# Bilinear einsum: the last weight group in three transfers of five, two and one rows instead of four transfers of four, two, one and one

## The chip, the cores and the metric

The kernel runs on one core of one Trainium2 chip. Times are microseconds of the device for one execution. A span, read from a profile, is about 1.3 us shorter than the time of the same execution. A ratio here is the mean time of one kernel's fast runs over that of the other kernel's fast runs of the same rounds, so it is not quite the ratio of the medians that are quoted. An interval is a 95% interval.

## The reference

```python
batch, dim_i, dim_j, dim_k = 32, 256, 256, 128      # all float32
out = np.einsum('bi,bj,kij->bk', x, y, weight)
```

The weight has 128 x 256 x 256 float32 values, 33.6 MB, and has to be read once. The other inputs and the output are small.

## The kernel before

The 128 values of k are cut into 32 groups of four. In a group, a partition holds one k and eight consecutive values of i, the eight "rows" of 256 weights. For each row one matmul multiplies by a block form of x and adds up in PSUM; after the eight rows VectorE multiplies with y and sums. The weights come by transfers that GpSimd issues and that convert to bf16 on the way (33.62 MB are read from HBM; the queue of these thirty groups moved 15.73 MB, half of their 31.46 MB of float32); two groups (0 and 16) come as float32 through another queue (2.11 MB). Each transfer has its own semaphore, and the first matmul that needs a row waits for it.

```python
LOADS = (
    ((8, 24), 0, 8),                  # groups, first row, row after the last
    ((4, 12, 20, 28), 0, 8),
    (tuple(range(2, 32, 4)), 0, 8),
    (tuple(range(1, 32, 4)), 0, 8),
    ((3, 11, 19, 27), 0, 8),
    ((7, 23), 0, 8),
    ((15,), 0, 8),
    ((31,), 0, 4),
    ((31,), 4, 6),
    ((31,), 6, 7),
    ((31,), 7, 8),
)
# ... cut ...
    sw = [
        nc.gpsimd.dma_start(
            out=w_of(groups)[:, :, lo * J:hi * J],
            in_=rows_of(groups)[:, :, lo * J:hi * J],
        ).then_inc(s, 16).ins
        for (groups, lo, hi), s in zip(LOADS, s_w)
    ]
# ... cut: all of these are issued at the start, back to back ...
            for g in unit[o:o + n]:
                s = sem_of.get((g, ic))
                if s is not None and s.num not in landed:
                    landed.add(s.num)
                    need.append(s)
# ... cut: the matmul of this row waits for what is in need ...
            done(v.tensor_tensor_reduce(
                out=prod[:, 0, :], in0=sums[:, 0, :], in1=y4, scale=1.0, scalar=0.0,
                op0=mult, op1=add, accum_out=acc[:, unit[0]:unit[0] + 1],
            )._wait_ge(s_pe, n_pe))
# ... cut ...
    sp.dma_start(out=out_v, in_=acc)._wait_ge(s_dve, n_dve).then_inc(s_out, 16)
```

Of the kernel before, what the change touches and what calls it, by code (L numbers as in the profile page):

```python
# [22 lines left out]
    ((3, 11, 19, 27), 0, 8),  # L23
    ((7, 23), 0, 8),
    ((15,), 0, 8),
    ((31,), 0, 4),
    ((31,), 4, 6),
    ((31,), 6, 7),
    ((31,), 7, 8),
)  # L30

# [315 lines left out]
```

## Time and profile before

| | before |
|---|---|
| time, median of 6 runs | 84.94 us (84.89 to 85.02) |
| span of the profiled execution | 83.4 us |
| TensorE busy, VectorE busy | 32.6 us (39%), 24.8 us (30%) |
| read from HBM | 33.62 MB, 404 GB/s over the span |
| transfers issued by GpSimd | 11 |

No compute engine is busy for half of the span, while the rate is nearly constant (203 to 218 GB/s written in slices 5 to 38 of 40); the prediction shows the slices and the chain of waits that say so. Two groups of the page are of use later. Their columns are: line, engine, operation, what it writes and reads, shapes, count; then busy us and mean ns of one; then the idle time of the engine before them, with what ended it.

```profile
L120 POOL DMA_DIRECT2D w_sb<-in_weight_dram x11 | 7.5, 700 | 0.6 <-issue 0.6
L301 DVE CUSTOM_DVE_ANT_0 tmp<-ps,y 128x256 f32<-128x256 f32 x2 | 0.9, 426 | 1.6 <-PE ps L236 1.4
```

The first says that issuing all eleven transfers keeps GpSimd busy for 7.5 us at the start. The second is the multiply-and-sum of groups 15 and 31; of its idle time, 1.4 us were spent waiting for TensorE's last matmul, so VectorE has that much to spare at the end.

### The profile page before, as it was taken

The page shows a single profiled execution, that of the slowest core. Times are in us where ns is not written, and L with a number is a line of the kernel's source. Part 1 is how long each engine was busy: PE and PEld are TensorE (multiplying, and loading weights), DVE is VectorE, ACT ScalarE, POOL GpSimd, SP SyncE. Part 2 cuts the span into 40 slices and gives each one's busy share as a digit, 9 for nine tenths or more (in the row PEclk, how much of TensorE's full clock was granted, in tenths as well). Part 3 has the DMA queues.
Part 4 walks back from the last instruction along what each step waited for, and adds up shares of the span by engine and source line. Part 5 has one row for each costly group of instructions (what it writes and reads, how often), then busy time and mean ns, then how long its engine had stood idle before and what let it go on. Part 6 is the DMA issues. An engine that isn't in the chain of part 4 may idle for free.

```text
span 83.4 us, 257 instructions
## 1 busy us (share of the span) xinstructions
PE 32.6 (39%) x136; PEld 4.3 (5%) x43; DVE 24.8 (30%) x28; ACT 5.3 (6%) x5; POOL 8.2 (10%) x17
## 2 busy tenths in 40 slices
PE   0000000000000000000099999997009999995780
PEld 0000000000000000000000000000000100112330
DVE  0038595000000000000000000002999900899932
ACT  0039830000000000000000000000000000000000
POOL 5999300000000000000000000000000000000000
PEclk9999999999999999999999999999995699999999
DMA  3999999999999999999999999999999999999980
GB/s 126 383 360 311 216 216 214 210 214 218 214 218 210 214 212 218 218 216 212 212 212 218 216 218 210 214 212 218 216 214 210 218 212 216 218 214 208 203 120 8
DMA packets 4928, 17.91 MB, mean 215 GB/s; under 512 B 384, under 2 KB 832, under 8 KB 4672
## 3 DMA queue, kind: packets, MB, share of 16 engines
q0 software_dynamic: 4400, 15.73, 94.3%
q1 hardware_dynamic: 432, 2.11, 6.7%
q10 hardware_dynamic: 96, 0.07, 0.3%
HBM read 33.62 MB, written 0.02 MB: 404 GB/s over the span
## 4 chain that ended last, share of the span: by engine, by line
DMA 47%; PE 39%; DVE 6%; another core or an unknown queue 2%; POOL 2%; issue 2%; POOLq 0%
DMA w_sb<-in_weight_dram 47%; PE ps L236 39%; DVE tmp L293 5%; POOL w_sb L120 2%; DVE tmp L301 1%; POOL const-float32-0.0 L331 0%; POOLq L331 0%; POOL const-uint8-127 L331 0%; POOL const-float32-1.0 L331 0%; DVE acc L301 0%
## 5 line engine op out<-in xcount | busy, mean ns | idle before, releaser
L236 PE MATMUL ps<-w_sb,xblk 128*128 128x512 bf16 (+1 forms) x136 | 32.6, 398 | 48.7 <-DMA w_sb<-in_weight_dram 43.9
L293 DVE TENSOR_TENSOR tmp<-ps,y 128x4096 f32<-128x4096 f32 (+3 forms) x4 | 8.6, 2153 | 48.4 <-PE ps L236 48.4
L297 DVE TENSOR_REDUCE acc<-tmp 128x16 f32<-128x4096 f32 (+3 forms) x4 | 8.6, 2155 | 0.1
L236 PEld LDWEIGHTS ps<-w_sb,xblk 128*128 128x128 bf16 x43 | 4.3, 101 | 76.9 <-DMA w_sb<-in_weight_dram 42.7
L120 POOL DMA_DIRECT2D w_sb<-in_weight_dram x11 | 7.5, 700 | 0.6 <-issue 0.6
L177 ACT CAST w_sb<-w_f 128x1024 bf16<-128x1024 f32 x4 | 4.0, 1042 | 0.4 <-DMA w_f<-in_weight_dram 0.4
L191 DVE COPY x_rep<-x_sb 32x1024 f32<-32x1024 f32 x1 | 0.7, 724 | 5.6 <-PEq L331 5.6
L226 DVE STREAM_TRANSPOSE y<-y_rep 32x256 f32<-32x256 f32 x4 | 1.7, 435 | 0.1
L197 DVE STREAM_TRANSPOSE xt<-x_rep 32x256 f32<-32x256 f32 x4 | 1.7, 434 | 0.1
L177 ACT ACT_TABLE_LOAD x1 | 1.3, 1283 | 5.5 <-PEq L331 5.5
L209 DVE TENSOR_SCALAR xblk<-xt,mask 128x256 bf16<-128x256 f32 x4 | 1.4, 501 | 0.0
L301 DVE CUSTOM_DVE_ANT_0 tmp<-ps,y 128x256 f32<-128x256 f32 x2 | 0.9, 426 | 1.6 <-PE ps L236 1.4
L221 DVE COPY y_rep<-yt 32x1024 f32<-32x1024 f32 x1 | 0.7, 682 | 0.0
L204 DVE TENSOR_REDUCE mask<-ident 128x4 f32<-128x128 f32 x1 | 0.4, 380 | 1.0 <-POOL ident L168 1.0
L218 DVE STREAM_TRANSPOSE yt<-y_sb 32x256 f32<-32x256 f32 x1 | 0.4, 446 | 0.0
L168 POOL TENSOR_SCALAR_AFFINE_SELECT ident<-ident 128x128 f32<-128x128 f32 x1 | 0.3, 287 | 0.1
L167 POOL MEMSET ident<- 128x128 f32 x1 | 0.3, 289 | 0.0
L301 DVE DVE_READ_ACCUMULATOR2_ANT acc<- 128x1 f32 x2 | 0.2, 84 | 0.0
L331 POOL MEMSET const-float32-0.0<- 128x1 f32 x1 | 0.1, 99 | 0.2 <-issue 0.2
L331 POOL MEMSET const-bfloat16-1.0<- 128x1 bf16 x1 | 0.1, 102 | 0.0
L331 POOL MEMSET const-uint8-127<- 128x1 uint8 x1 | 0.1, 102 | 0.0
L331 POOL MEMSET const-float32-1.0<- 128x1 f32 x1 | 0.1, 99 | 0.0
## 6 DMA issues: line engine op xcount, KB each, us to landing
w_sb<-in_weight_dram POOLq DMA_DIRECT2D x2, 4096.0 KB, 48.5
w_sb<-in_weight_dram POOLq DMA_DIRECT2D x2, 2048.0 KB, 43.6
w_f<-in_weight_dram SPq DMA_DIRECT2D x2, 1024.0 KB, 6.9
w_sb<-in_weight_dram POOLq DMA_DIRECT2D x2, 1024.0 KB, 41.2
w_sb<-in_weight_dram POOLq DMA_DIRECT2D x1, 512.0 KB, 72.6
w_sb<-in_weight_dram POOLq DMA_DIRECT2D x1, 256.0 KB, 73.3
w_sb<-in_weight_dram POOLq DMA_DIRECT2D x1, 128.0 KB, 73.4
w_sb<-in_weight_dram POOLq DMA_DIRECT2D x2, 64.0 KB, 73.1
```

Of the source, the lines that this page charges most:

```text
L120: nc.gpsimd.dma_start(out=w_of(groups)[:, :, lo * J:hi * J], in_=rows_of(groups)[:, :, lo * J:hi * J],).then_inc(s, 16).ins
L177: c = act.copy(out=w_sb[:, place_of[g], lo:hi], in_=w_f[:, n, lo:hi])
L191: t = done(v.tensor_copy(out=x_rep, in_=x_sb.rearrange("b (ip ic) -> b ic ip", ic=IC).unsqueeze(3) .to_broadcast([B, IC, IP, KK]),)._wait_ ...
L197: c = v.transpose(out=xt[q * 32:(q + 1) * 32, :, :], in_=x_rep[:, :, q * IP // Q:(q + 1) * IP // Q, :],)
L204: t = done(v.tensor_reduce(out=mask, in_=ident.rearrange("p (ip kk) -> p kk ip", kk=KK), axis=AX, op=add,)._wait_ge(s_pool, 2))
L209: c = v.tensor_scalar(out=xblk[:, :, :, kk], in0=xt, scalar1=mask[:, kk:kk + 1], scalar2=None, op0=mult,)
L221: t = done(v.tensor_copy(out=y_rep, in_=yt.unsqueeze(3).to_broadcast([B, J // 32, B, KK]),)._wait_ge(s_dve, t))
L226: c = v.transpose(out=y4[q * 32:(q + 1) * 32, :].rearrange("p (jb j) -> p jb j", j=32), in_=y_rep[:, :, q * BQ:(q + 1) * BQ, :],)
L236: return pe.add_instruction(mybir.InstMatmult(name=nc.get_next_instruction_name(), engine=mybir.EngineType.PE, ins=[pe.lower_ap(rhs), pe.l ...
L293: t = done(v.tensor_tensor(out=prod, in0=sums, in1=y4.unsqueeze(1).to_broadcast([P, n_g, J]), op=mult,)._wait_ge(s_pe, n_pe))
L297: done(v.tensor_reduce(out=acc[:, unit[0]:unit[-1] + 1:unit[1] - unit[0]], in_=prod, axis=AX, op=add,)._wait_ge(s_dve, t))
L301: done(v.tensor_tensor_reduce(out=prod[:, 0, :], in0=sums[:, 0, :], in1=y4, scale=1.0, scalar=0.0, op0=mult, op1=add, accum_out=acc[:, uni ...
```

## The change

The intent is to save one transfer on a stream that does not rest (the DMA engines are at 90% or more in slices 2 to 38 of 40), while the last transfer stays small, so that little work is left when it lands.

```diff
     ((15,), 0, 8),
-    ((31,), 0, 4),
-    ((31,), 4, 6),
-    ((31,), 6, 7),
+    ((31,), 0, 5),
+    ((31,), 5, 7),
     ((31,), 7, 8),
 )
```

## The prediction

The sum came to minus 0.047 us, from 85.0 to 84.95 us.

> **What bounds the kernel now.** I first read the busy shares by slice, to see which resource never rests, and then the chain of work that ended last, in order of time, to see what sets the end. The page of the kernel before has this:
>
> ```profile
> PE   0000000000000000000099999997009999995780
> ...
> PEclk9999999999999999999999999999995699999999
> DMA  3999999999999999999999999999999999999980
> GB/s 126 383 360 311 216 216 214 210 214 218 214 218 210 214 212 218 218 216 212 212 212 218 216 218 210 214 212 218 216 214 210 218 212 216 218 214 208 203 120 8
> ```
>
> Each digit is a slice of 83.4 / 40 = 2.1 us. The DMA engines are full from the second slice to the thirty-eighth; TensorE starts half way and has gaps afterwards. The rate counts what is written, in bf16; what is read is float32, twice that, so the flat 210 to 218 GB/s is about 430 GB/s of reading. The kernel is a weight stream, and its time is the stream, plus what must be done after its last byte.
>
> That tail is the last part of the chain (start in us, length in us, what):
>
> ```profile
> 74.81 1.19 another core or an unknown queue
> 76.00 0.04 issue
> 76.04 1.89 PE ps L236 x8
> 77.93 0.53 another core or an unknown queue
> 78.46 0.04 issue
> 78.50 1.03 PE ps L236 x8
> 79.53 0.18 another core or an unknown queue
> 79.71 0.04 issue
> 79.75 0.60 PE ps L236 x4
> 80.35 0.06 another core or an unknown queue
> 80.41 0.05 issue
> 80.45 0.59 PE ps L236 x3
> 81.04 0.01 another core or an unknown queue
> 81.06 0.05 issue
> 81.10 0.30 PE ps L236
> 81.40 0.02 issue
> 81.42 0.43 DVE tmp L301
> ```
>
> There is only one core, so "another core or an unknown queue" is not that. Every one of these waits is TensorE waiting for a weight transfer that was issued about 73 us earlier, too long ago for the view to tie them together; the matmuls that end them are the ones that carry a wait on a piece's semaphore. So the start of each "issue" line is the moment at which a piece has landed: groups 7 and 23 at 76.00, group 15 at 78.46, then of group 31 rows 0 to 3 at 79.71, rows 4 and 5 at 80.41, and row 7 at 81.06. Row 6 does not show as a wait in the chain; the weight load that opens it starts at 80.75 in the order of instructions, so it landed at about 80.71. (A "row" is one of the eight rows of 256 weights that a partition holds of a group: 128 x 256 x 4 = 131,072 bytes read, one matmul.) After 81.06 come 0.04 of wake-up, the last matmul, the multiply-and-sum on VectorE, and the store, which ends the span at 83.4, that is 2.3 us later.
>
> [...] the fit below gives 131,072 B in 0.302 us, 434 GB/s. [...] Here the pieces are queued behind each other[...]: two one-row pieces landed within 0.65 us together. [...] (eight take 1.03 us, and one by itself 0.27: 0.76 / 7 = 0.109). [...] the digits 5 and 6 in the clock row are one such half-speed stretch in this trace.
>
> **The change part by part.** It removes one transfer (pieces 4, 2, 1, 1 become 5, 2, 1), one semaphore and one wait of TensorE. The bytes, the 136 matmuls, their order, VectorE's work and the store stay, which the comparison of the two programs' instructions per engine confirms: the only difference beside line numbers is one DMA fewer on GpSimd's queue.
>
> What a piece costs on the stream: group 15 is eight rows in one piece, 78.46 - 76.00 = 2.46 us. Group 31 is the same eight rows in four pieces, 81.06 - 78.46 = 2.60 us. Three more pieces cost 0.14 us, so **a piece costs 0.047 us**, and a row (2.46 - 0.047) / 8 = 0.302 us. Check: four rows give 4 x 0.302 + 0.047 = 1.25 (seen 79.71 - 78.46 = 1.25); two rows 0.65 (seen 0.70); two pieces of one row 0.70 (seen 0.65). Single landings scatter by 0.05 around the fit, but their sum holds.
>
> The new landings follow, as estimates from these two numbers:
> - rows 0 to 4: 78.46 + 5 x 0.302 + 0.047 = 80.02
> - rows 5 and 6: 80.02 + 2 x 0.302 + 0.047 = 80.67
> - row 7: 80.67 + 0.302 + 0.047 = 81.01 or 81.02, against 81.06
>
> What TensorE does with them, with 0.04 us from landing to start and 0.109 us from one matmul to the next: rows 0 to 4 start between 80.06 and 80.50, and TensorE could take row 5 at 80.61; it lands at 80.67 and starts at 80.71, row 6 at 80.82, and TensorE could take row 7 at 80.93. Row 7 starts only when it has landed, at 81.06. So the last piece still ends the chain, with 0.13 us to spare; before, row 6 started at 80.75, row 7 could have gone at 80.86, and went at 81.10, 0.24 us to spare. The larger first piece eats 0.11 us of slack, not of time. After row 7's start everything is as before.
>
> The sum on the path that sets the end: **minus 0.047 us** for one piece, and nothing else. The wait removed on TensorE (0.04 or 0.05 us of wake-up) lay in time that TensorE had to spare. On GpSimd one issue fewer saves about 0.55 to 0.7 us (eleven issues took 548 to 884 ns, median 696) at about 8 us; it brings forward the identity, VectorE's mask and the block weights by up to that, but TensorE waits for weights until 41.9 us, so none of it reaches the end. 85.0 - 0.05 gives 84.95 us.
>
> **The rivals.**
>
> First: a piece costs much more than 0.047 us, [...] the 0.2 us that one would get by adding up packet times. [...] I give it little.
>
> Second: the coarser first piece turns the tail from waiting for DMA to waiting for TensorE. Five matmuls begin 0.31 us later than four did. If TensorE ran at half its clock in the last 1.5 us, 256 columns would take 0.22 us each, and the eight matmuls, from 80.06, would start the last at 80.06 + 7 x 0.22 = 81.6, that is 0.5 us later than now: 85.5 us. In this trace the clock is full from slice 33 on, and the half-speed stretch (matmuls at half rate in about 62.8 to 66.2 us) is far ahead of the tail with a second one only after the last matmul. [...] the three runs before, within 0.13 us, show no such outlier. At full clock this rival is worth 0 us, since 0.13 us of slack remain.
>
> Third: the change is worth nothing at all, because the 0.14 us is not a cost of pieces but of the stream's end [...]. Then the time stays at 85.0. For it: the 0.14 us includes the last landing, and I cannot split it. Against it: the four-row piece, which has others behind it, already carries 0.04 us over its bytes, and the two-row piece 0.10. A mixture is possible, anything between 0 and 0.05 us saved.
>
> Fourth: a five-row write is 2560 bytes per partition[...] and may be cut into two packets. Nothing in the trace has this size; the one-row pieces, with the smallest packets, kept within 0.05 us of the fit, so a few more packets would cost 0.05 us at most: 85.0.
>
> **Range and chances.** All but the second rival lie between 84.8 and 85.05 us; the three runs before spread from 84.89 to 85.02, so the noise of a median is about as large as the effect, which I do not expect to be visible in three runs. I take 84.95, with 84.77 to 85.13: the effect of 0 to 0.1 plus 0.1 on each side for the runs and the chip. A change by 2% is 1.7 us, 36 times the estimate; a whole 2% faster or slower needs something that no view shows. Faster 0.005, within 2% 0.99, slower 0.005.
>
> **What would show it.** In the chain of the changed kernel the tail should have three waits for pieces of the last group where there were four pieces; rows 0 to 4 should land 1.56 us after group 15, and row 7 2.55 us after it in place of 2.60. Landing to end should stay 2.3 us. The first step is wrong if the last landing comes the same 2.60 us after group 15 (third rival) or under 2.45 (first rival); the second is wrong if the last matmul follows the one before it by 0.11 us and not after a wait. The prediction as a whole falls if the median moves by more than 0.2 us.

The 0.109 us is the step from one 128x256 matmul to the next in group 15 (0.108 or 0.109 us in the records). In the half-speed stretch of 62.8 to 66.2 us the 128x512 matmuls start 0.427 us apart, as do the first ones, up to 45.7 us; the others, back to back, 0.216; the 0.22 us for 256 columns is the estimate, twice 0.109. The 0.2 us of packet times can be had from the packet records: 60 ns for one of 512 B, 98 for 1024, 173 for 2048, 324 for 4096, and 22 for each of the sixteen packets of 4 B that come with a transfer. Over 16 engines this adds up to 3.22 us for group 31 in four pieces and to 2.61 for group 15 in one, 0.20 us for each of the three more. At that cost the time would fall to about 84.8 us, an estimate; against it stands that group 31 took 0.14 us longer than group 15, and not 0.6.

## The result, and the profile after

| | before | after |
|---|---|---|
| time, median of 6 runs each | 84.94 us (84.89 to 85.02) | 84.85 us (84.72 to 85.18) |
| ratio, interval | | 0.9993, 0.9975 to 1.0011 |
| span of the profiled execution | 83.4 us | 83.6 us |

The time is within 2%, and in the range. The profiled span nevertheless grew, which has to be explained. First the slices of the changed kernel, from its page:

```profile
PE   0000000000000000000089999999106999998770
PEclk9999999999999999999999999999965579999999
DMA  4999999999999999999999999999999999999960
GB/s 102 389 354 320 223 214 210 218 218 214 214 218 210 216 216 218 212 218 218 206 218 218 214 216 218 216 208 218 218 214 214 220 208 214 218 214 214 202 104 8
```

The stream is as full as before (202 to 220 GB/s in slices 6 to 38). The stretch in which TensorE had half its clock is longer (the digits 6, 5, 5, 7): the trace's clock records, which say 0.50, put it at 61.1 to 67.9 us, 6.8 us long, where the kernel before had 62.8 to 66.2, 3.4 us. Next the tail of the chain of waits (start, length, what), where the prediction showed that of the kernel before:

```profile
63.32 12.79 PE ps L235 x48
76.10 0.18 another core or an unknown queue
76.28 0.04 issue
76.33 1.89 PE ps L235 x8
78.21 0.54 another core or an unknown queue
78.75 0.04 issue
78.80 1.03 PE ps L235 x8
79.83 0.47 another core or an unknown queue
80.30 0.04 issue
80.34 1.30 PE ps L235 x8
81.64 0.02 issue
81.67 0.43 DVE tmp L300
```

Groups 7 and 23 land at 76.28 in place of 76.00, group 15 at 78.75 in place of 78.46: the whole stream ran 0.29 us late before it came to the first changed transfer. Rows 0 to 4 of group 31 then landed 80.30 - 78.75 = 1.55 us later. The other two pieces do not show here as waits, because the modelled end of the fifth matmul (81.05) lies past the landing of the second piece (80.99). They show in the order of the weight loads, each of which comes just before its matmul (start, length, engine, line, operation, count, and in brackets the idle time and what ended it):

```profile
80.34 0.42 PEld L235 LDWEIGHTS ps<-w_sb,xblk 128*128 128x128 bf16 x4 [0.79 <-issue]
81.03 0.11 PEld L235 LDWEIGHTS ps<-w_sb,xblk 128*128 128x128 bf16 x2 [0.27 <-DMA w_sb<-in_weight_dram]
81.34 0.10 PEld L235 LDWEIGHTS ps<-w_sb,xblk 128*128 128x128 bf16 x1 [0.19 <-DMA w_sb<-in_weight_dram]
```

Row 5 and row 7 both begin when a transfer has landed; TensorE waited for each. The trace also records every increment of a semaphore, and every weight transfer has sixteen of them; its landing can be given to the nanosecond as the sixteenth. These are from those records:

```
us from the start of the span           before    after
groups 8 and 24 (first GpSimd transfer) 12.557    12.844
groups 7 and 23                         75.997    76.285
group 15                                78.458    78.753
group 31, last piece                    81.057    81.298
end of the span                         83.351    83.583
group 15 to last piece                   2.599     2.545
last piece to end                        2.294     2.285
first GpSimd landing to end             70.794    70.739
```

The tail shrank by 0.054 us. The 0.29 us by which this execution was late were already there at its first GpSimd landing, 66 us before group 15 landed and the first changed transfer had the stream. The last row takes that lateness away, and is the measure that I use for the experiments: it says what a kernel does once its stream runs.

Two groups of the page answer to the two shown of before:

```profile
L119 POOL DMA_DIRECT2D w_sb<-in_weight_dram x10 | 7.1, 722 | 0.6 <-issue 0.6
L300 DVE CUSTOM_DVE_ANT_0 tmp<-ps,y 128x256 f32<-128x256 f32 x2 | 0.8, 420 | 0.3 <-PE ps L235 0.3
```

GpSimd was done 0.4 us sooner. VectorE's spare time at the end fell from 1.4 to 0.3 us, since the longer half-speed stretch had delayed the units ahead of the last (in the second trace of the changed kernel, below, where the stretch lasted 3.4 us, VectorE's last wait was 1.4 us again); it is a slack that was used, not time lost.

### The profile page after: what moved, and what is told of

Its sections match the earlier page's. It is cut to its first block, busy times and chain, and to the rows that moved or that the text cites. A ratio compares the mean times of both kernels' runs of the same rounds, so it can differ in the third digit from the quotient of the medians.

```text
span 83.6 us, 256 instructions
## 1 busy us (share of the span) xinstructions
PE 33.6 (40%) x136; PEld 4.3 (5%) x43; DVE 24.7 (30%) x28; ACT 5.3 (6%) x5; POOL 7.8 (9%) x16
## 2 busy tenths in 40 slices
DMA packets 4784, 17.91 MB, mean 214 GB/s; under 512 B 368, under 2 KB 688, under 8 KB 4528
## 4 chain that ended last, share of the span: by engine, by line
DMA 47%; PE 40%; DVE 6%; POOL 2%; another core or an unknown queue 1%; issue 1%; POOLq 0%
DMA w_sb<-in_weight_dram 47%; PE ps L235 40%; DVE tmp L292 5%; POOL w_sb L119 2%; DVE tmp L300 1%; POOL const-float32-0.0 L330 0%; POOLq L330 0%; POOL const-uint8-127 L330 0%; POOL const-float32-1.0 L330 0%; DVE acc L300 0%
## 5 line engine op out<-in xcount | busy, mean ns | idle before, releaser
L235 PE MATMUL ps<-w_sb,xblk 128*128 128x512 bf16 (+1 forms) x136 | 33.6, 410 | 48.0 <-DMA w_sb<-in_weight_dram 43.5
```

What stands on the lines that cost most here:

```text
L235: return pe.add_instruction(mybir.InstMatmult(name=nc.get_next_instruction_name(), engine=mybir.EngineType.PE, ins=[pe.lower_ap(rhs), pe.l ...
```

## The experiments

The theory: a transfer costs the stream about 0.05 us wherever it stands, the bytes cost the rest, and the end follows the last landing as long as TensorE is not behind. The rivals: the 0.05 us belong to the end of the stream, or are scatter (pieces cost nothing); or it is TensorE, not the landing, that ends the tail. Twelve more runs followed, on three chips; each is compared with the kernel before on its own chip. All gave correct results. "Rest" is from the first GpSimd landing to the end of the span, in the one profiled execution.

```
kernel            pieces of group 31   first   rest    median   ratio    interval
                                       landing
before            4 2 1 1              12.56   70.79   84.94
after             5 2 1                12.84   70.74   84.85    0.9993   0.9975-1.0011
before_again      4 2 1 1              12.64   70.79   84.98    0.9998   0.9978-1.0018
after_again       5 2 1                12.67   70.75   84.72    0.9975   0.9957-0.9994
after_third       5 2 1                12.83   70.74   84.87    0.9999   0.9983-1.0016
six_one_one       6 1 1                12.73   70.79   84.96    1.0009   0.9988-1.0029
seven_one         7 1                  12.80   71.08   85.34    1.0047   1.0027-1.0066
one_piece         8                    13.18   71.40   85.91    1.0118   1.0085-1.0152
one_piece_again   8                    12.72   71.39   85.56    1.0081   1.0064-1.0098
one_piece_ten     8, and loads cut     12.97   71.43   85.68    1.0114   1.0069-1.0159
eight_pieces      1 x 8                13.01   70.97   85.33    1.0050   1.0026-1.0074
eight_whole       5 2 1, load cut      13.03   70.91   85.32    1.0040   1.0019-1.0060
g15_eight         5 2 1, group 15 cut  12.77   71.68   85.81    1.0101   1.0084-1.0117
four_by_rows      5 2 1, load cut      13.01   75.28   90.02    1.0604   1.0579-1.0628
```

### Both kernels again

The changed kernel, without an edit:

> The changed kernel once more (5, 2, 1). Theory: a piece costs the stream 0.047 us, so the last piece of group 31 lands 2.55 us after group 15 (2.53 to 2.57), the last matmul starts 0.04 us after that, and the time is 0.05 us under the kernel before (ratio 0.9994), inside the noise. Rival, pieces cost nothing and the 2.60 us of the kernel before is the end of the stream: 2.60 us again in most traces and no difference in the time. Second rival, a throttled clock makes TensorE the last to finish: the last matmul starts more than 0.1 us after the last landing.

The kernel before, without an edit:

> The kernel before once more (4, 2, 1, 1), for its trace. Theory: last piece lands 2.60 us after group 15 (2.58 to 2.62), ratio 1.000. If the landings scatter so that 2.55 comes up here, the 0.05 us between the two kernels is scatter and the theory has no footing. Where group 15 itself lands should scatter from trace to trace by some 0.3 us, as between the two traces already seen (78.46 and 78.75), which would say why the profiled span grew though the tail shrank.

And the changed kernel on another chip:

> The changed kernel a third time. From the group 15 landing to the last landing 2.545 us (2.53 to 2.56) as in both traces so far; from the landing of the first GpSimd transfer (groups 8 and 24) to the end of the span 70.74 us (70.70 to 70.78), against 70.79 in both traces of the kernel before. If the change is worth only this 0.05 us, the median is within 0.15 us of before and the ratio near 0.9994; the 0.9975 of the last time was then the start of the stream, which differs from execution to execution. If the change is worth 0.2 us, 0.9975 comes up again.

From group 15 to the last landing the changed kernel took 2.545, 2.546 and 2.553 us in its three traces, the kernel before 2.599 and 2.600. From the first landing to the end they took 70.74, 70.75 and 70.74 against 70.79 and 70.79. So the 0.05 us repeat to within 0.01 us as long as the kernel has ten transfers from GpSimd; the section on every fourth transfer shows that their number matters too. The times do not resolve them: the changed kernel came out at 0.9993, 0.9975 and 0.9999 of before. The expected 0.9994 lies inside the first and the third interval and at the edge of the second. Group 15 landed at 78.46, 78.54, 78.58, 78.73 and 78.75 us in the five traces, which is the 0.3 us of scatter expected. The second rival is out in all three traces: the last matmul started 0.046 or 0.047 us after the last landing.

### How many pieces

```diff
-    ((31,), 0, 5), ((31,), 5, 7), ((31,), 7, 8),
+    ((31,), 0, 8),                                   # one_piece
+    ((31,), 0, 1), ((31,), 1, 2), ... ((31,), 7, 8), # eight_pieces
```

> Group 31 in one piece. Theory: it lands 8 x 0.302 + 0.047 = 2.46 us after group 15, the earliest of all; but then eight matmuls follow, 7 x 0.109 = 0.76 us from the first start to the last, so the last matmul starts 2.46 + 0.04 + 0.76 = 3.27 us after group 15's landing in place of 2.64 before: 0.62 us slower than before, about 85.55, ratio 1.0073. Rival, the transfer's end is all that matters: 0.14 us faster than before, ratio 0.998.

> Group 31 in eight pieces of one row. Theory: four pieces more than before, last landing 8 x (0.302 + 0.047) = 2.79 us after group 15, last matmul 0.04 us later, 0.19 us slower than before: about 85.1, ratio 1.0022. Rival, a piece costs nothing (end of the stream only): 2.60 us, ratio 1.000 or below. Rival, a piece costs far more than 0.047 us once there are many: more than 3.0 us, ratio over 1.005.

From group 15 to the last landing: one piece 2.450 us, three 2.546, four 2.600, eight 2.800. That is close to a straight line of (2.800 - 2.450) / 7 = 0.050 us a piece, from one to eight (two pieces, which ran later, lie 0.05 us above it; see below); the rival in which pieces cost nothing is out here, and so is the one in which they cost much more. With one piece the last landing comes earliest and the kernel is slower all the same. This is the end of its chain:

```profile
80.15 1.38 another core or an unknown queue
81.52 0.04 issue
81.56 1.05 PE ps L233 x8
82.61 0.02 issue
82.64 0.42 DVE tmp L298
```

All eight matmuls of the group lie after the landing, 1.05 us in place of the 0.30 of one. The last matmul started 82.326 - 79.074 = 3.25 us after group 15 (estimated 3.27), and the rest is 71.40 - 70.79 = 0.61 us longer than before (estimated 0.62).

The times of the two kernels missed: 0.94 us (85.91 - 84.97) and 0.36 us (85.33 - 84.97) over before, where 0.62 and 0.19 were expected. The rest of the profiled executions was longer than before by the 0.61 and 0.18 us expected, but their first landings were late, at 13.18 and 13.01 us, and not at 12.6. To see if that belonged to the one-piece kernel, it ran again, and in a form with ten transfers as the changed kernel has:

> One piece again, for the 0.3 us that it was slower than its tail explains. Its part from the first GpSimd landing to the end should again be 71.40 us. If the excess belongs to the start of single executions, the first landing comes at 12.5 to 12.9 us this time and the ratio is 1.007 to 1.009; if it belongs to this kernel, the landing is again near 13.2 and the ratio near 1.012.

> One piece for group 31, with ten transfers as in the changed kernel: two loads of eight whole groups are cut into two of four. The stream pays two completions, 2 x 0.019 = 0.04 us; from the first landing to the end 71.44 us. If few issues on GpSimd were what made the start of the one-piece kernel late, the first landing is near 12.7 and the ratio near 1.008; if not, it is like that of the one-piece kernel beside it.

```diff
-    (tuple(range(2, 32, 4)), 0, 8),
-    (tuple(range(1, 32, 4)), 0, 8),
+    ((2, 10, 18, 26), 0, 8), ((6, 14, 22, 30), 0, 8),
+    ((1, 9, 17, 25), 0, 8), ((5, 13, 21, 29), 0, 8),
```

The second time, on another chip, the one-piece kernel's first landing was at 12.72 us and its ratio 1.0081; the rest was 71.39 us again. So the late start does not belong to that kernel. The form with ten transfers had the rest expected (71.43 us for 71.44), and its first landing at 12.97, later than that of the one-piece kernel beside it: nothing here, in one trace each, speaks for few issues on GpSimd as what makes a start late. What does is open: in the latest one the slowest increments of the float32 load of group 0 were already late, at 5.91 us against 5.24 in the trace of before, ahead of any landing from GpSimd. The clock is open too: three of the six runs of the one-piece kernel (85.95 to 86.47 us) and two of the six with ten transfers (86.18 and 86.63) show a mean clock of 0.937 to 0.942, where no run of the kernel before is under 0.959. None of these was profiled, so it is not known whether half-speed matmuls fell into their tails, where this kernel has eight.

### How large the first piece may be

```diff
-    ((31,), 0, 5), ((31,), 5, 7), ((31,), 7, 8),
+    ((31,), 0, 6), ((31,), 6, 7), ((31,), 7, 8),     # six_one_one
+    ((31,), 0, 7), ((31,), 7, 8),                    # seven_one
```

> Pieces of six, one and one: as many as in the changed kernel. Last landing 2.545 us after group 15 as there, but six rows land at 1.85, and TensorE, at 0.109 us a row from 1.89, reaches row 7 only at 1.89 + 7 x 0.109 = 2.65: the last matmul starts 0.06 us later than in the changed kernel (2.59), where it started in the kernel before. From the first landing to the end 70.80 us. Rival, the number of pieces alone counts: 70.74.

> Group 31 in two pieces, seven rows and one. Theory: last landing 8 x 0.30 + 2 x 0.05 = 2.50 us after group 15, earlier than in either kernel; but seven rows land at 2.15, and their seven matmuls start from 2.19 to 2.84, so TensorE ends the chain: the last matmul starts 2.95 us after group 15's landing, not 0.04 us after its own piece, in place of 2.59 in the changed kernel. So 0.36 us slower than the changed kernel, 0.31 slower than before (ratio about 1.0035). Rival, fewer pieces are better whatever their size: last matmul at 2.54, ratio 0.998.

With six rows first, the last landing came 2.557 us after group 15, as with five, but the rest was 70.79 us, back at the kernel before (expected 70.80). With seven, the last landing came 2.546 us after group 15 (expected 2.50; the section on every fourth transfer says why), and the last matmul 2.96 us after it (expected 2.95), so the rest grew to 71.08. The weight loads of the two kernels, six_one_one first, show that there is no wait left between the rows:

```profile
80.52 0.79 PEld L235 LDWEIGHTS ps<-w_sb,xblk 128*128 128x128 bf16 x7 [1.11 <-issue]
```

```profile
80.90 0.75 PEld L234 LDWEIGHTS ps<-w_sb,xblk 128*128 128x128 bf16 x7 [1.41 <-issue]
```

In the changed kernel the same view has three lines, two of them begun by a landing. Here TensorE runs through, one matmul in 0.109 us, and ends the chain. Of the sizes that ran, five rows are the most that the first piece held without a loss.

### Where the 0.05 us sits

Group 15 has other transfers behind it, so it tells whether only the end of the stream pays; cutting a load into whole groups adds completions but no packet of weights (eight_whole counts 4896 packets, 112 more than the changed kernel, which is sixteen under 512 B for each of its seven transfers more); cutting one by rows adds both (four_by_rows counts 8480, 3696 more: the 112, and 3584 of weights).

```diff
-    (tuple(range(1, 32, 4)), 0, 8),
+    *(((g,), 0, 8) for g in range(1, 32, 4)),                # eight_whole
-    ((15,), 0, 8),
+    *(((15,), r, r + 1) for r in range(8)),                  # g15_eight
-    ((3, 11, 19, 27), 0, 8),
+    *(((3, 11, 19, 27), r, r + 1) for r in range(8)),        # four_by_rows
```

> The load of eight whole groups (1, 5, ... 29) cut into eight transfers of one whole group; packets stay the same (one of 4096 bytes for each partition and group), only seven completions are added. From the traces so far: eight groups in one transfer take 19.52 to 19.53 us, one alone 2.457 on average, which gives about 0.019 us for a transfer's completion and 0.0038 us for each packet on a DMA engine (8 packets and a completion make the 0.05 us of a one-row piece). Theory, both count: this load takes 19.52 + 7 x 0.019 = 19.65 us. Rival, all is in the completion: 19.87. Rival, all is in the packets: 19.52. Time: 85.0 (84.85 to 85.15) under the theory.

> Last group as in the changed kernel (5, 2, 1), but group 15, which is not at the end of the stream, in eight transfers of one row. Theory: the cost of a piece is a cost of the stream anywhere in it, so group 15 takes 2.80 us from the landing of groups 7 and 23 in place of 2.45 to 2.47, group 31 still 2.55, and the time grows by 7 x 0.05 = 0.35 us over the changed kernel: about 85.2, ratio to the kernel before about 1.0035. Rival, only the end of the stream pays for pieces: group 15 stays at 2.46 and the time is unchanged, ratio 0.999.

> The load of groups 3, 11, 19, 27 cut by rows into eight transfers: 32 packets of 512 bytes a DMA engine in each, so 256 packets and eight completions in place of 32 and one. Theory (0.0038 us a packet, 0.019 us a completion): 9.82 us grow by 224 x 0.0038 + 7 x 0.019 = 0.98 to about 10.80, and the time by about as much, to 85.85, ratio 1.011. Rival, all in the completion: 10.17 and ratio 1.004. Rival, all in the packets (0.05 / 8 = 0.0063 us each): 11.2 and ratio 1.016.

The load in eight whole groups took 61.932 - 42.272 = 19.66 us, for 19.65 expected if a completion costs 0.019 us, 19.52 if it costs nothing and 19.87 if it costs everything. So completions pay a part, about two fifths of a one-row piece's 0.05 us. The time missed all the same: 85.32 us, where 84.85 to 85.15 were expected. The rest is 0.17 us longer than in the changed kernel, of which the seven completions are 0.14, and the first landing was late again, at 13.03 us. The 0.0038 us a packet remains an estimate of the fit; no run here shows it by itself.

The other two refuted the rival that only the end pays, but missed their own numbers. Group 15 in eight pieces took 3.36 us (79.558 - 76.199), not 2.80, and the rest grew by 0.94 us and not by 0.35. The four groups by rows took 14.20 us (75.986 - 61.787) and not 10.80, and the time rose by 6% where 1.1% was expected. The rate of that kernel, in the same slices as on the other pages, falls in the middle of the stream:

```profile
GB/s 85 387 372 295 215 217 217 213 212 213 221 213 212 215 219 213 212 215 217 217 212 213 219 217 212 213 213 198 151 156 185 188 196 192 209 212 204 103 32 7
```

The sixteen increments of a piece's semaphore, which I take for one from each of the 16 engines that the page counts (the trace does not show it), say how: until that load they lay within 0.76 us of each other. In its last piece eight of them came within 0.34 us of the first, and eight 1.7 to 3.8 us after it. The earliest of the sixteen took 72.169 - 61.065 = 11.10 us, near the estimate; the other half of the increments came far later, and a transfer has landed only when the slowest has. So 0.05 us a piece holds for the last group, where it was fitted and repeated up to eight pieces, and is no constant of the stream. In group 15 the excess is not spread over the pieces: the first took 0.73 us (group 31's first: 0.36) and the last 0.51, the six between 2.12 / 6 = 0.35, which is a row and 0.05 us. Why eight one-row pieces cost 2.80 us in group 31 and 3.36 in group 15, and why half of the increments fell behind, stays open; the trace does not say which engine a packet ran on.

### Every fourth transfer

The landing records of these runs show one more regularity. In the twelve traces other than those of group 15 in eight pieces and of the four groups by rows, I compared each of the 56 landings of pieces of one group, counted from the landing before it, with 0.301 us a row and 0.047 us a piece (the best fit, found together with the 0.04 us below). 31 of them agree within 0.014 us. The 13 that end with the 5th, 9th, 13th or 17th transfer that GpSimd issued come 0.02 to 0.05 us later, 0.04 on average, and the 12 that follow one of these are shorter by as much: such a transfer lands late, but the stream behind it does not.

This explains what was put down to scatter. The prediction's two-row piece (0.70 us seen, 0.65 fitted) is the 9th transfer. So is the last one of the kernel with seven rows and one: 2.546 us for 2.50. In the three kernels with 17 transfers, whose last group is cut into 5, 2 and 1 as in the changed kernel, the 17th is the last: it landed 2.583, 2.595 and 2.576 us after group 15, and not 2.55. So an otherwise equal tail can lose nearly all of the 0.05 us by the number of transfers alone. The semaphores are numbered in the order of the transfers, so the traces cannot tell whether it goes by order or by semaphore; the cause is open, and no run was made to test it.

## Why the prediction was right

- **The cost of a piece** was put at 0.047 us from one trace; a line through one, three, four and eight pieces gives 0.050, and the fit over 56 landings 0.047. Some of that was luck: the landings that it took, of group 15 and of the last row, are those of the 7th and the 11th transfer, and the last of the changed kernel is the 10th, so none of them is a late fourth one. The reading of "another core or an unknown queue" as landings, on which this rested, agrees with the semaphore records.
- **The landings**: rows 0 to 4 were to land 1.56 us after group 15 and did after 1.54, 1.55 and 1.57; row 7 was to land after 2.55 and did after 2.545 to 2.553.
- **TensorE's slack** at row 7 was to be 0.13 us. In the trace after, row 6 started at 81.157 and row 7 at 81.345; at 0.109 us a row it could have started at 81.266, so 0.08 us were left; the two-row piece, the 9th transfer, had landed 0.03 us later than predicted (2.238 us after group 15). That the first piece eats slack and not time was right, and the six-row kernel shows how little more it may eat.
- **The sum**, minus 0.047 us, came out as 0.054 in the tail and 0.05 in the rest. The time, 84.85, lies in the range, but the 0.09 us between the two medians are no proof of it: the changed kernel's own medians lie between 84.72 and 84.87.
- **GpSimd's issue** was to save 0.55 to 0.7 us off the path. It saved 0.4, since ten issues took 722 ns each and not 700; VectorE's first copy had 5.2 us of idle time before it in place of 5.6. That none of it reaches the end held: TensorE's first matmul starts when the weights land, at 42.1 us.
- **The rivals.** The first and the third fell with the straight line of pieces, the third for the middle of the stream too. What the prediction held against the third was weaker than it looked: of the two-row piece's 0.10 us over its bytes, 0.04 is the lateness of a 9th transfer. The fourth fell by count: 128 packets of 512 B and one transfer's 16 of 4 B fewer make 4928 - 144 = 4784, which is what the page counts, and the packet records have 128 of 2560 B, so five rows are one packet. The second did not come about in the tail. But the half-speed stretch did double in the profiled execution, where I had looked only at a stretch that would fall into the last 1.5 us. It used up slack ahead of it: TensorE's wait for groups 7 and 23 shrank from 1.19 to 0.18 us and VectorE's spare time from 1.4 to 0.3. It is not of the change's making: the second trace of the changed kernel has a stretch of 3.4 us, and these waits were 1.20 and 1.4 us there; and a mean clock of 0.959 for an execution, which goes with 6.8 us in the profiled ones, came in 8 of 11 runs of the kernel before, and 0.98 in the other 3.
- **The rate**: that more is not to be had was not shown. Measured are 131,072 B in 0.302 us, 434 GB/s of reading, half of which, 217 GB/s, is written; what limits this was not tested. Nothing else in the prediction needs it, since a row's 0.302 us is measured.
- **Wrong in what would show it**: the chain was to have three waits for pieces of group 31. It has one; the other two show only among the weight loads, for the reason given with the chain.
- **Not foreseen**: the start of the stream differs by 0.3 us and more from one execution to the next (the first GpSimd landing came between 12.56 and 13.18 us in fourteen traces), six times the effect, and made the profiled span longer while the tail became shorter.

Of the splits that ran, five, two and one has the shortest rest. No experiment points to one that would beat it by more than the scatter of the start.

## What to carry to other kernels

When a stream of transfers sets the time, cut its last part so that each piece lands just as the compute engine is done with the one before: fewer pieces save about 0.05 us each here, but a piece too large puts 0.109 us of matmul for every row behind the last landing, and both limits can be worked out from one trace. Compare such kernels from an event inside the stream to the end, not by the whole span, when the start scatters more than the effect (here 0.6 us over fourteen traces, for an effect of 0.05). A cost fitted at one place (0.05 us a piece) need not hold for the same pieces elsewhere in the stream (eight one-row pieces took 2.80 us in group 31 and 3.36 in group 15); test it there first. Count the transfers as well: here every fourth landed 0.04 us late, as much as a piece costs.
